# RWKV-7 pair of head groups: in each level's stint all products first, the reads of their PSUM banks behind them, and another order of asking for the banks

## The chip, the core and the metric

The kernel runs on one NeuronCore of a Trainium2 chip. The metric is device time in microseconds (us) from one launch, the median of several runs. TensorE is called PE here, VectorE DVE, ScalarE ACT, GpSimd POOL, SyncE SP. "PEld" is PE's loading of the stationary operand.

## The reference

One decoder block over 256 tokens of width 2048: an input projection, two token mixers side by side (RWKV-7 with 16 heads of 64, and an mLSTM), gates, an output projection, a layer norm, then a mixture of 32 experts and a second layer norm. The change touches the RWKV-7 recurrence only:

```python
def _rwkv7_scan(r, decay, k, v, kk, a):
    # S_t = S_{t-1} (diag(w_t) - kk_t^T (a_t * kk_t)) + v_t^T k_t ;  y_t = S_t r_t
    def step(state, inp):
        r_t, w_t, k_t, v_t, kk_t, a_t = inp
        s_kk = jnp.einsum('bhvk,bhk->bhv', state, kk_t)
        state = (state * w_t[:, :, None, :]
                 - s_kk[..., None] * (kk_t * a_t)[:, :, None, :]
                 + v_t[..., None] * k_t[:, :, None, :])
        return state, jnp.einsum('bhvk,bhk->bhv', state, r_t)
    ...
# and around it
    u = x @ w_in[i]
    y_r = _rwkv7_mixer(u_r, ...); y_m = _mlstm_mixer(u_m, ...)
    mix = (sigmoid(g_r) * (y_r @ w_br[i]) + sigmoid(g_m) * (y_m @ w_bm[i])) @ w_out[i]
    x = _layer_norm(ALPHA * x + mix, ...)
    moe = _hier_moe(x, ...)            # top-1 of 4 groups, top-2 of its 8 experts
    x = _layer_norm(ALPHA * x + moe + ple, ...)
```

## The kernel before

**The front.** The projections run as weight steps on PE. A step takes 256 KB of weights that SP has loaded, ACT rounds them to a high part (line 224) and DVE takes the remainder as a low part (line 225), four steps ahead of PE (`AHEAD = 4`), and PE multiplies by the high part (line 289, 512 columns) and by the low part (line 290, 256 columns), four pairs of L289 and L290 in a step around the change. SP loads the next weights when a raw buffer has been split.

**The mixers in between.** The recurrence and the mLSTM are generators. After each weight step `advance()` first lets a finished projection's evacuation do one piece (L364 on ACT, L366 on DVE, L376 to L378, L940), then runs the next piece of the mixer in front, up to its `yield n`; `n` is how many weight steps pass before the next piece. Such a piece is called a stint here. The order on every engine is therefore the order in which the code is written; nothing reorders it later, and each engine works through its own queue in that order. A tile framework puts in the semaphore waits, by tile of PSUM or SBUF.

**The pair.** The 16 heads are four groups of four heads; the 256 tokens are four chunks of 64. For each group `opening(g)` prepares, for every chunk and head, a 64x64 triangular matrix (`BA`) and a first approximation `Tm` of the inverse of identity plus that matrix. `closing(a, b)` then takes two groups as a pair and doubles the exact block size of the inverse five times for each, in ten levels k = 0 to 9: even k for group a, odd k for group b. A level has two halves, and its second half is done in the stint of the next level, beside the first half of the other group's level:

- first half of level k: 16 products `BA` x `Tm` of 64x64 into columns 0 to 255 of two banks `X[0]`, `X[1]` (L570); four transposes of `Tm` into a bank `pz` (L583); a copy of `pz` to `Gm` by ACT (L584); and a masked copy of the products to `M1` by DVE, one instruction for each bank (L586).
- second half of level k-1: 16 products `Gm` x `M1` into columns 256 to 511 of the same two banks (L562), and `Tm -= ` these, one DVE instruction for each bank (L565).

In levels 0 and 1 there are 16 more products into a bank `px` (L578) with a copy `Xs` by ACT (L580). In the stint k = 10 only the second half of level 9 is left, and the first part of `ending(a)` follows in the same stint: for q = 0 and then q = 1 products into `P[q]` (L608, L613), which ACT and DVE read (L615, L616). There are two pairs, so each of these stints occurs twice in a run. `Gm` and `M1` exist once; `Tm` exists once for each group of the pair (B_66 and B_63 in the rows below).

**The banks.** `bank()` takes the next of four PSUM banks in turn (`bufs=4`); a bank's new owner waits until the old owner's readers are through. `bank2()` gives the projections two double banks of their own (`dps`).

Of a stint's code the order before was: ask for `X[0]` and `X[1]`; products L562; the two subtractions L565; products L570; in levels 0 and 1 products L578 and copy L580; ask for `pz`; transposes L583; copy L584; masks L586.

Of the kernel before, what the change touches and what calls it, by code (L numbers as in the profile page):

```python
# [14 lines left out]
AF = mybir.ActivationFunctionType  # L15
OP = mybir.AluOpType
# [96 lines left out]
def _carve(t, off, *dims, p0=0, p1=128):  # L113
    n = int(np.prod(dims))
    ap = t[p0:p1, off:off + n]
    if len(dims) > 1:
        names = "abcde"[:len(dims)]
        ap = ap.rearrange("p (%s) -> p %s" % (" ".join(names), " ".join(names)),
                          **{m: d for m, d in zip(names, dims)})
    return ap  # L120
# [3 lines left out]
def hybrid_block(ctx: ExitStack, tc: tile.TileContext, xt, xp, vec, cst, sel8, rows, ln1c, pt, w_lora, w_rkv, w_qk,  # L124
                 w_mv, w_o, w_gt, lw, lg1, w_br, w_bm, w_out, ifb, w_rt, b_rt, w_gu0, w_gu2, w_dn, w_pg, out):
    nc = tc.nc
    pe, act, dve, pool, sp = nc.tensor, nc.scalar, nc.vector, nc.gpsimd, nc.sync
# [8 lines left out]
    def bank():  # L136
        return ps.tile([128, 512], FT, name="mps", tag="m", bufs=4)


    def big(i, dt=FT):  # L140

        return sb.tile([128, 4096], dt, name=f"B{i}", tag=f"B{i}")
# [13 lines left out]
    def cst_(name, w=None, o=0):  # L156
        return C[:, _CST[name] + o:_CST[name] + o + (w or 128)]
# [188 lines left out]
    sets = [{n: _carve(*h[n], *d) for n, d in dims.items()} for h in (homes_a, homes_b)]  # L346
# [53 lines left out]
    def evac_mixed(g, w):  # L400

        name, lock, old = (("mu_r", "zr", g - 1), ("mu_k", "zr", g - 1), ("mu_v", "zv", g - 2))[w]
        dst = (zr, zk, zv[:, g % 2])[w]

        def f(p_):
            t = yield from total_slow(p_)
            while free[lock] < old:
                yield
            for c in range(2):
                (shift_chunks if w == 2 else shift_mix)(dst[:, :, c] if w == 2 else dst[:, c], t[:, c],  # L410
                                                        *vm(name, 2 * g + c))
                yield
            if w == (1 if g else 2):
                mixers.append(opening(g))
                if g % 2:
                    mixers.append(closing(g - 1, g))
        return f
# [5 lines left out]
    quarter = lambda p_, o=0: p_[:, o:o + 256].rearrange("p (j n) -> p j n", n=64)  # L423
# [128 lines left out]
    def closing(a, b):  # L552

        ends = [ending(g) for g in (a, b)]
        for k in range(11):
            X = bank(), bank()
            up, down_ = (sets[(k + i) % 2] for i in range(2))
            if k:
                Tm = down_["Tm"]
                for j in range(4):  # L560
                    for c, q in quads:
                        mm(X[q][half[c], 256 + 64 * j:320 + 64 * j], Gm[half[q], j, c, :], M1[half[q], c, j, :],  # L562
                           start=True, stop=True)
                for q in range(2):
                    dve.tensor_tensor(Tm[:, :, q], Tm[:, :, q], quarter(X[q], 256), op=OP.subtract)  # L565
            if k < 10:
                Tm, BA, Xs, vN = (up[n] for n in ("Tm", "BA", "Xs", "vN"))
                for j in range(4):
                    for c, q in quads:
                        mm(X[c][half[q], 64 * j:64 * j + 64], BA[half[c], q, j, 2, :], Tm[half[c], j, q, :], start=True,  # L570
                           stop=True)
                if k < 2:
                    px = bank()
                    for q in range(2):
                        for j in range(4):
                            for c in range(2):
                                o = 256 * q + 64 * j
                                mm(px[half[c], o:o + 64], BA[half[c], q, j, 0, :], vN[half[c], j, half[q]], start=True,  # L578
                                   stop=True)
                    act.activation(Xs.rearrange("p q j n -> p (q j n)"), px, AF.Copy)  # L580
                pz = bank()
                for j in range(4):
                    pe.transpose(pz[:, 128 * j:128 * j + 128], tok(Tm, j), ident)  # L583
                act.activation(Gm.rearrange("p j c n -> p (j c n)"), pz, AF.Copy)  # L584
                for c in range(2):
                    dve.tensor_tensor(M1[:, c], quarter(X[c]), bc(cst_("lv", 64, k // 2 * 64), 4), op=OP.mult)  # L586
                yield Y_LV[k]
            else:
                yield next(ends[0])
        while ends:  # L590
            w = 0
            for e in list(ends):
                n = next(e, 0)
                if not n:
                    ends.remove(e)
                w = max(w, n)
            if w:
                yield w

    def ending(g):  # L600
# [77 lines left out]
        flat8 = lambda a: a.rearrange("p b n -> p (b n)")  # L678
        dve.tensor_reduce(flat8(mean), y, axis=AX.X, op=OP.add)
        dve.tensor_scalar(mean, mean, -1.0 / 64, None, op0=OP.mult)  # L680
# [4 lines left out]
        yield next(wait)  # L685
        dve.tensor_reduce(flat8(rstd), ysq.rearrange("p s h n -> p (s h) n"), axis=AX.X, op=OP.add)
        yield next(wait)
# [558 lines left out]
    x1 = _carve(big(8), 0, 2, 2048)  # L1246
# [567 lines left out]
    for e in range(NE - 2):  # L1814
        g, i = (e + 2) // 4, (e + 2) % 4
# [17 lines left out]
        if over:  # L1833
            pz, ph = pu2[:, 1], pu[:, 0, 256:384]
# [231 lines left out]
```

## Time and profile before

| | us |
|---|---|
| median of 3 runs | 1771.89 (1770.75 to 1774.1) |
| the profiled execution | 1773.26 |
| its span, first to last instruction | 1771.5 |
| PE busy | 1570.8 (89%) |
| DVE busy | 788.2 (44%) |
| ACT busy | 601.8 (34%) |
| granted PE clock, mean | 0.953 |
| first pair's stints k = 0 to 10 | from 176.9 on |
| second pair's last stint k = 10 | starts at 417.99 |

In the timeline a row gives the start in us, the duration in us, engine, line, operation, output and inputs, shapes and the number of instructions merged; a bracket gives the idle time of the engine ahead of it and what ended it. Each 64x64 product stands there as two matrix instructions, so 16 products read "x32". The ends of matrix instructions are modelled, so the steps between starts say more than durations.

### The profile page before, as it was taken

What the parts mean: (1) busy time and instruction counts of PE and PEld (TensorE: products, weight loads), DVE (VectorE), ACT (ScalarE), POOL (GpSimd) and SP (SyncE); (2) the same over time, 40 slices, a digit from 0 to 9 for tenths busy, and PEclk for the clock granted to TensorE, in tenths of its full rate; (3) what the DMA queues carried; (4) which work ended last, traced back from release to release, by engine and by line L of the source; (5) the groups of instructions that cost most, each with busy time, mean ns of one, the idle gap of its engine ahead of it and who ended that gap; (6) DMA issues with size and microseconds to landing.
All of it is one profiled execution on the core that took longest, in us unless ns stands there. A gap on an engine that the chain in (4) does not pass through costs nothing. (4 is left out here: it accounts for less than half of the span.)

```text
span 1771.5 us, 35255 instructions
## 1 busy us (share of the span) xinstructions
PE 1570.8 (89%) x14589; PEld 1090.5 (62%) x14589; DVE 788.2 (44%) x1655; ACT 601.8 (34%) x1122; POOL 25.1 (1%) x39
## 2 busy tenths in 40 slices
PE   7999899999999999999898878797887879877886
PEld 6888788877888888776465455364555334433332
DVE  5577578765775787755231201221201312321315
ACT  5656357643765565444121011111011111111122
POOL 1000000000000000000000000000000000000002
PEclk9999999999999999999999998899999899988888
DMA  7554235432566448867999999999999999999997
GB/s 239 174 167 152 83 113 174 151 111 73 160 187 201 148 149 332 323 226 300 428 425 427 425 426 426 395 428 425 426 426 427 424 425 392 428 424 426 425 427 323
DMA packets 68767, 542.09 MB, mean 306 GB/s; under 512 B 7796, under 2 KB 12292, under 8 KB 42704
## 3 DMA queue, kind: packets, MB, share of 16 engines
q1 hardware_dynamic: 67728, 537.33, 77.1%
q8 instruction: 146, 2.39, 0.6%
q0 software_dynamic: 832, 1.87, 0.4%
q14 instruction: 61, 0.50, 0.1%
HBM read 537.06 MB, written 2.36 MB: 304 GB/s over the span
## 5 line engine op out<-in xcount | busy, mean ns | idle before, releaser
L289 PE MATMUL dps<-B,B 128*128 128x512 f32 x1456 | 530.4, 406 | 11.9 <-DVE B L1204 11.2
L290 PE MATMUL dps<-B,B 128*128 128x256 f32 x1456 | 412.4, 283 | 4.8 <-DVE B L225 4.4
L225 DVE TENSOR_TENSOR B<-B,B 128x512 fp32r<-128x512 f32 (+1 forms) x464 | 312.6, 683 | 195.1 <-ACT B L224 191.0
L224 ACT ACTIVATE B<-B 128x512 fp32r<-128x512 f32 (+1 forms) x464 | 283.6, 622 | 156.9 <-PE dps L289 67.2
L289 PEld LDWEIGHTS dps<-B,B 128*128 128x128 f32 x1456 | 276.7, 190 | 79.7 <-ACT B L224 9.1
L1514 PE MATMUL dps<-B,B 128*32 128x256 f32 x3936 | 252.3, 414 | 64.3 <-DMA B<-in_w_up_dram 29.6
L290 PEld LDWEIGHTS dps<-B,B 128*128 128x128 f32 x1456 | 278.3, 191 | 12.7 <-DVE B L225 10.3
L1514 PEld LDWEIGHTS dps<-B,B 128*32 128x32 f32 x3936 | 134.8, 118 | 185.5 <-issue 43.7
L1519 DVE SCALAR_TENSOR_TENSOR M<-M,dps 128x128 f32<-128x128 f32 x31 | 8.9, 288 | 368.9 <-ACT M L1518 368.9
L1908 ACT ACTIVATE B<-mps 32x512 f32<-32x512 f32 x120 | 70.6, 588 | 180.6 <-PE mps L1534 179.5
L1534 PE MATMUL mps<-B,M 128*32 128x512 f32 x992 | 125.0, 644 | 6.9 <-DMA B<-in_w_down_dram 2.5
L1311 PE MATMUL mps<-B,B 128*128 128x206 f32 (+1 forms) x640 | 112.8, 336 | 0.3 <-DVE B L1300 0.3
L1311 PEld LDWEIGHTS mps<-B,B 128*128 128x128 f32 x640 | 110.6, 190 | 1.4 <-issue 0.8
L1518 ACT ACTIVATE M<-dps 128x128 f32<-128x128 f32 x31 | 8.6, 278 | 270.6 <-PE dps L1514 270.6
L1534 PEld LDWEIGHTS mps<-B,M 128*32 128x32 f32 x992 | 31.0, 116 | 82.6 <-issue 71.5
L297 PE MATMUL dps<-B,B 128*128 128x512 f32 x192 | 76.1, 397 | 1.2 <-DVE B L988 0.8
L299 PE MATMUL dps<-B,B 128*128 128x512 f32 x192 | 75.1, 391 | 0.7 <-DVE B L225 0.7
L298 PE MATMUL dps<-B,B 128*128 128x512 f32 x192 | 74.8, 390 | 0.0
L1590 DVE TENSOR_TENSOR B<-mps,V 128x512 f32<-128x512 f32 (+1 forms) x34 | 21.9, 643 | 86.5 <-PE mps L1584 86.5
L1554 PE MATMUL mps<-B 128*128 128x512 f32 (+1 forms) x128 | 56.7, 595 | 0.7 <-ACT B L1908 0.7
L1514 PE MATMUL dps<-B,C 128*32 128x256 f32 x768 | 46.9, 401 | 7.6 <-DVE C L1591 7.6
L1324 DVE SCALAR_TENSOR_TENSOR C<-C,mps 128x412 f32<-128x412 f32 (+1 forms) x10 | 5.8, 581 | 102.1 <-PE mps L1316 92.0
(511 smaller groups left out, 1554.1 us busy)
## 6 DMA issues: line engine op xcount, KB each, us to landing
B<-in_w_gate_dram SPq DMA_DIRECT2D x62, 2048.0 KB, 19.5
B<-in_w_up_dram SPq DMA_DIRECT2D x61, 2048.0 KB, 21.9
B<-in_w_down_dram SPq DMA_DIRECT2D x60, 2048.0 KB, 21.2
B<-in_w_gt_dram SPq DMA_DIRECT2D x64, 512.0 KB, 3.6
B<-in_w_rkv_dram SPq DMA_DIRECT2D x48, 512.0 KB, 3.6
B<-in_w_pg_dram SPq DMA_DIRECT2D x10, 1854.0 KB, 29.5
B<-in_w_out_dram SPq DMA_DIRECT2D x32, 512.0 KB, 3.8
B<-in_w_qk_dram SPq DMA_DIRECT2D x16, 512.0 KB, 3.6
```

Of the source, the lines that this page charges most:

```text
L224: act.activation(h, src, AF.Copy)
L225: dve.tensor_tensor(wl[i % 4][:, :w], src, h.bitcast(FT), op=OP.subtract)
L289: mm(pt_[:, c], h[:, w], x.rearrange("p a t -> p (a t)"), start=k == 0, stop=False)
L290: mm(pt_[:, c, :256], l[:, w], x[:, 0], start=False, stop=k == nk - 1)
L297: mm(o, mh[:, ts_], h, start=first, stop=False)
L298: mm(o, ml[:, ts_], h, start=False, stop=False)
L299: mm(o, mh[:, ts_], l, start=False, stop=last)
L1311: mm(pp[:, tb], x1T[0][:, k, tb * 128:tb * 128 + 128], w[:, k, :n], start=k == 0 and tb == 0, stop=k == 15 and tb == 1)
L1514: mm(pu[32 * j:32 * j + 32].rearrange("p (a f) -> p a f", a=2), xs[:, 4 * q + k, :], o, start=q == QS[0] and k == 0, stop=q == QS[-1] and ...
L1534: mm(pd[32 * j:32 * j + 32, :], hT_[:, 32 * c:32 * c + 32], w[:, c % 2, 512 * j:512 * j + 512], start=c == 0, stop=c == 3)
L1554: mm(pz, SWT[p0:p1, tb * 128:tb * 128 + 128], yq[p0:p1, o], start=True, stop=True)
L1908: act.activation(yq[32 * i:32 * i + 32, 512 * j:512 * j + 512], pd[32 * j:32 * j + 32, :], AF.Copy)
```

## The change

The stint's code is put in another order, and the three banks are asked for in the order `X[0]`, `pz`, `X[1]`, in all stints, k = 10 too (where `pz` is then not used). All products of a stint (L562, L568 that was L570, L576 that was L578) and the transposes (L579, was L583) come first; then the copy `Gm` (L580, was L584), the masks `M1` (L582, was L586), in levels 0 and 1 the copy `Xs` (L584, was L580), and the two subtractions last (L588, was L565). No instruction is added or removed.

```diff
         for k in range(11):
-            X = bank(), bank()
-            up, down_ = (sets[(k + i) % 2] for i in range(2))
+            x0, pz, x1 = (bank() for _ in range(3))
+            X = x0, x1
+            up, last = (sets[(k + i) % 2] for i in range(2))
             if k:
-                Tm = down_["Tm"]
                 for j in range(4):
                     for c, q in quads:
                         mm(X[q][half[c], 256 + 64 * j:320 + 64 * j], Gm[half[q], j, c, :], M1[half[q], c, j, :],
                            start=True, stop=True)
-                for q in range(2):
-                    dve.tensor_tensor(Tm[:, :, q], Tm[:, :, q], quarter(X[q], 256), op=OP.subtract)
             if k < 10:
                 Tm, BA, Xs, vN = (up[n] for n in ("Tm", "BA", "Xs", "vN"))
                 for j in range(4):
...
                                 mm(px[half[c], o:o + 64], BA[half[c], q, j, 0, :], vN[half[c], j, half[q]], start=True,
                                    stop=True)
-                    act.activation(Xs.rearrange("p q j n -> p (q j n)"), px, AF.Copy)
-                pz = bank()
                 for j in range(4):
                     pe.transpose(pz[:, 128 * j:128 * j + 128], tok(Tm, j), ident)
                 act.activation(Gm.rearrange("p j c n -> p (j c n)"), pz, AF.Copy)
                 for c in range(2):
                     dve.tensor_tensor(M1[:, c], quarter(X[c]), bc(cst_("lv", 64, k // 2 * 64), 4), op=OP.mult)
+                if k < 2:
+                    act.activation(Xs.rearrange("p q j n -> p (q j n)"), px, AF.Copy)
+            if k:
+                for q in range(2):
+                    Tm = last["Tm"]
+                    dve.tensor_tensor(Tm[:, :, q], Tm[:, :, q], quarter(X[q], 256), op=OP.subtract)
+            if k < 10:
                 yield Y_LV[k]
             else:
                 yield next(ends[0])
```

PE's queue in the stint k = 4 of the first pair, with the engines whose semaphores a row waits for, before:

```order
L562 MATMUL mps<-B_66 64x64 [waits DVE_49,Activation_49]
L562 MATMUL mps<-B_66 64x64 [waits PE_49]
L562 MATMUL mps<-B_66 64x64 [waits DVE_49]
L562 MATMUL mps<-B_66 64x64 x13
L570 MATMUL mps<-B_66,B_68 64x64 [waits DVE_49]
L570 MATMUL mps<-B_66,B_68 64x64
L570 MATMUL mps<-B_66,B_68 64x64 [waits DVE_49]
L570 MATMUL mps<-B_66,B_68 64x64 x13
L583 MATMUL mps<-C,B_66 128x128 [waits PE_49]
```

and now:

```order
L562 MATMUL mps<-B_66 64x64 [waits DVE_49,Activation_49]
L562 MATMUL mps<-B_66 64x64 [waits PE_49]
L562 MATMUL mps<-B_66 64x64 [waits DVE_49]
L562 MATMUL mps<-B_66 64x64 x13
L568 MATMUL mps<-B_66,B_68 64x64 [waits DVE_49] x2
L568 MATMUL mps<-B_66,B_68 64x64 x14
L579 MATMUL mps<-C,B_66 128x128 x4
```

The order of PE's work is the same. The first products into each bank waited for DVE in the same stint (the subtraction of that bank); the DVE wait that is left at L568 is for DVE work that stands ahead of this stint's products: the subtraction that wrote this group's `Tm` one stint earlier.

DVE's queue in the stint k = 7 of the first pair, as a difference (`-` before, `+` now):

```order
 L225 TENSOR_TENSOR B_70<-B_69,B_70 128x512 [waits Activation_49]
 L366 TENSOR_TENSOR R<-R,dps 128x512
-L565 TENSOR_TENSOR B_66<-B_66,mps 128x4x64 [waits PE_49] x2
-L586 TENSOR_TENSOR B_66<-mps,C 128x256 [waits DVE_49,PE_49] x2
+L582 TENSOR_TENSOR B_66<-mps,C 128x256 [waits DVE_49,PE_49] x2
+L588 TENSOR_TENSOR B_66<-B_66,mps 128x4x64 x2
 L225 TENSOR_TENSOR B_70<-B_69,B_70 128x512 [waits DMAHW1_49,Activation_49]
 L377 SCALAR_TENSOR_TENSOR B_63<-R,V,B_63 128x4x63 [waits Activation_49]
```

The two masks now stand ahead of the two subtractions; what stands ahead of and behind the four is the same.

PE's queue in the stint k = 10 of the first pair, before:

```order
L562 MATMUL mps<-B_66 64x64 x13
L608 MATMUL mps<-B_68,B_66 64x64 [waits PE_49]
L608 MATMUL mps<-B_68,B_66 64x64 x7
L613 MATMUL mps<-B_66 64x64 [waits DMAHW7_49]
L608 MATMUL mps<-B_68,B_66 64x64 [waits PE_49]
```

and now:

```order
L562 MATMUL mps<-B_66 64x64 x13
L611 MATMUL mps<-B_68,B_66 64x64 [waits DVE_49]
L611 MATMUL mps<-B_68,B_66 64x64 x7
L616 MATMUL mps<-B_66 64x64 [waits DMAHW7_49]
L611 MATMUL mps<-B_68,B_66 64x64 [waits DVE_49]
```

Both halves q = 0 and q = 1 of the ending's first products now wait for DVE. With the third bank asked for in this stint, `P[1]` gets the bank of `X[0]`, which this stint's first subtraction reads; `P[0]` waits for `Tm`, written one stint earlier.

## The prediction

> **What bounds the kernel now.** I read the page first, for where the time of the changed stints lies.
>
> ```profile
> span 1771.5 us, 35255 instructions
> PEclk9999999999999999999999998899999899988888
> DMA  7554235432566448867999999999999999999997
> ```
>
> The stints lie in the fifth, sixth, ninth and tenth slice. There the DMA engines are busy 2 to 4 tenths and PE has its full clock. I then cut the span into stretches (busy us and count of PE, PEld, DVE, ACT, POOL; granted PE clock, DMA share, GB/s).
>
> ```profile
> 176.90:226.50 49.60, 43.77 (x907) 36.30 (x907) 26.40 (x60) 17.64 (x33) 0.00 (x0) 1.00 0.25 76
> 380.00:430.00 50.00, 45.40 (x970) 37.71 (x966) 26.38 (x59) 16.89 (x31) 0.00 (x0) 1.00 0.23 73
> 430.00:760.00 330.00, 322.55 (x1990) 273.18 (x1982) 239.58 (x472) 190.79 (x346) 1.23 (x4) 0.99 0.61 208
> 760.00:1771.50 1011.50, 843.83 (x8175) 477.29 (x8173) 260.91 (x643) 176.30 (x348) 14.17 (x14) 0.92 0.97 406
> ```
>
> Up to 760 us PE sets the pace: 322.55 of 330 us busy behind the pairs, less only in the pairs themselves. From 760 us on the weights' stream does (DMA share 0.97). So time won by PE in a pair brings all of the front forward, and with it the start of the stream. What PE waits for in the pairs stands in the waits (total us, times, longest) and the groups:
>
> ```profile
> PE mps L570 <- DVE B L565: 11.0, 18, 0.9
> L570 PE MATMUL mps<-B,B 64*64 64x64 f32 x640 | 19.5, 227 | 11.0 <-DVE B L565 11.0
> ```
>
> 18 waits: k = 1 to 9 in both pairs. Since the ends of PE's instructions are modelled, 11.0 need not be the whole loss, and I measured from start to start. All engines in the stint k = 3:
>
> ```profile
> 192.37 0.69 DVE L225 TENSOR_TENSOR B<-B,B 128x512 fp32r<-128x512 f32 x1 [1.12 <-ACT B L224]
> 192.44 0.69 PE L562 MATMUL mps<-B 64*64 64x64 f32 x32
> 193.19 0.75 DVE L565 TENSOR_TENSOR B<-B,mps 128x256 f32<-128x256 f32 x2
> 193.66 1.01 PE L570 MATMUL mps<-B,B 64*64 64x64 f32 x32 [0.53 <-DVE B L565]
> 194.61 0.66 PE L583 MATMUL mps<-C,B 128*128 128x128 f32 x4
> 194.64 0.76 DVE L586 TENSOR_TENSOR B<-mps,C 128x256 f32<-128x256 f32 x2 [0.70 <-PE mps L570]
> 195.36 0.60 ACT L584 ACTIVATE B<-mps 128x512 f32<-128x512 f32 x1 [3.03 <-PE mps L583]
> 195.86 0.62 ACT L224 ACTIVATE B<-B 128x512 fp32r<-128x512 f32 x1
> 196.51 0.69 DVE L225 TENSOR_TENSOR B<-B,B 128x512 fp32r<-128x512 f32 x1 [1.12 <-ACT B L224]
> 196.59 0.69 PE L562 MATMUL mps<-B 64*64 64x64 f32 x32
> ```
>
> L562 runs, DVE subtracts from the first bank, and only then may L570 write there; its second bank waits for the second subtraction, which stretches L570 to 1.01. L562 to L583 takes 2.17 us, and the whole stint with its weight step 4.15.
>
> **The change part by part.** *The products.* What two sets of products take with nothing between them is shown where no subtraction stands: at k = 0 (L570, L578, L583) and at k = 10 (L562, L608, L613).
>
> ```profile
> 176.91 0.69 PE L570 MATMUL mps<-B,B 64*64 64x64 f32 x32
> 177.42 1.11 PE L578 MATMUL mps<-B,B 64*64 64x64 f32 x32
> 178.47 0.66 PE L583 MATMUL mps<-C,B 128*128 128x128 f32 x4
> 222.48 0.69 PE L562 MATMUL mps<-B 64*64 64x64 f32 x32
> 222.99 0.65 PE L608 MATMUL mps<-B,B 64*64 64x64 f32 x16
> 223.29 0.75 DVE L565 TENSOR_TENSOR B<-B,mps 128x256 f32<-128x256 f32 x2
> 223.81 0.65 PE L608 MATMUL mps<-B,B 64*64 64x64 f32 x16
> 224.27 0.53 PE L613 MATMUL mps<-B 64*64 64x64 f32 x12
> 224.73 0.50 PE L289 MATMUL dps<-B,B 128*128 128x512 f32 x1
> ```
>
> From 16 undisturbed products of 0.69 us to the next 64x64 products it is 0.51 us (176.91 to 177.42, 222.48 to 222.99). To the 128x128 work behind them it is longer: L578, of 1.11, starts 1.05 ahead of L583, and L613, of 0.53, 0.46 ahead of L289, so 0.06 to 0.07 below the duration, which makes 0.62 after 0.69. (The new pair of neighbours, L568 and L579, has no row: the ends are 0.51, as among 64x64 products, and 0.69, the whole duration; 0.62 is from the nearest rows.) A stint k = 2 to 9 then takes 0.51 + 0.62 = 1.13 from L562 to the transposes, and k = 1, with L576 (was L578) between, 0.51 + 0.51 + 1.05 = 2.07.
>
> *Beside it, the page "TensorEngine Tiling (Array Packing)" of the Trainium skill says under Key Properties that a change of tiling mode drains PE. The rows above agree: 0.62 into the 128x128 work against 0.51 within 64x64. By a chip without that drain the 16 stints would each give 0.11 more, 1.8 us in all.*
>
> What these stints take now, besides k = 3: the last of the 16, the k = 1 of the first pair, and the four whose wait is longer than 0.53.
>
> ```profile
> 413.84 0.69 PE L562 MATMUL mps<-B 64*64 64x64 f32 x32
> 416.01 0.66 PE L583 MATMUL mps<-C,B 128*128 128x128 f32 x4
> 181.83 0.69 PE L562 MATMUL mps<-B 64*64 64x64 f32 x32
> 184.93 0.66 PE L583 MATMUL mps<-C,B 128*128 128x128 f32 x4
> 210.65 1.01 PE L570 MATMUL mps<-B,B 64*64 64x64 f32 x32 [0.90 <-DVE B L565]
> 215.10 1.01 PE L570 MATMUL mps<-B,B 64*64 64x64 f32 x32 [0.84 <-DVE B L565]
> 219.55 1.01 PE L570 MATMUL mps<-B,B 64*64 64x64 f32 x32 [0.83 <-DVE B L565]
> 406.76 1.01 PE L570 MATMUL mps<-B,B 64*64 64x64 f32 x32 [0.91 <-DVE B L565]
> ```
>
> Twelve take 2.17; the four take 0.37, 0.31, 0.30 and 0.38 more, since evacuation work of DVE stood ahead of the subtraction. Together 16 x 2.17 + 1.36 = 36.1. Now 16 x 1.13 = 18.1, which leaves **18.0**. The two k = 1: 2 x (3.10 - 2.07) = **2.1**.
>
> *DVE's order.* Masks first, subtractions behind. With T the start of the transposes (k = 3: 194.61), the masks start at T + 0.03, both subtractions end at about T + 0.03 + 0.76 + 0.75 = T + 1.54. The next stint's L562 comes, as before, 1.98 after T (194.61 to 196.59), its L568 at T + 2.49. L562 needs the masks (T + 0.79) and `Gm` (T + 0.75 + 0.60 = T + 1.35); L568 needs the subtractions. All are early, by 0.6 us at the least. The weights' split comes behind, as before: L225 starts at T + 1.90, when DVE is just free. What the new period of 1.98 + 1.13 = 3.11 us must hold on DVE is 0.75 + 0.76 + 0.69 = 2.2 us, in a stint with an evacuation up to 0.7 more (the row below), which fits. Cost 0; if this cover were gone, PE would stand at L568 with the transposes and the next step's L289 queued behind, and ACT's L224, which waits for freed weight buffers, behind those.
>
> ```profile
> L366 DVE TENSOR_TENSOR R<-R,dps 128x512 f32<-128x512 f32 x24 | 16.3, 680 | 0.8 <-ACT R L364 0.8
> ```
>
> *ACT's order.* In levels 0 and 1 `Gm` comes ahead of `Xs`, 0.6 us earlier than now; two weight steps follow, so nobody feels it. `Xs` is read in the ending only. No DMA moves against the steps, and nothing on POOL.
>
> *Banks.* `pz` of a stint gets the bank of the last stint's `X[0]`, whose reader ended at T + 1.54 at the latest, 1.5 us ahead of the transposes. At k = 10 the products for q = 1 get this stint's `X[0]` bank: the subtraction starts at 223.29 and its first half ends some 0.4 later, 0.1 ahead of the second L608 at 223.81. Hidden here with little to spare; bound 0 to 0.7 (one L366 ahead of it), twice; I take 0.
>
> Sum: 18.0 + 2.1 = **20.1 us**, between 17 (0.15 in each of the 18 stints and 0.4 at the two k = 10 together given back; 0.69 in place of 0.62 alone costs 1.1) and 21.9 (0.51 in place of 0.62). The profiled execution took 1773.26, 1.8 more than its span, which makes 1753.2; the runs' median is 1.4 lower, 1771.89, which makes **1751.8**, and I say 1752.
>
> **The rivals.** *Only the listed wait goes* (0.08): 11.0 us, 1760.9. That would be so if L570's 1.01 and L562's 0.69 were their own pace. The k = 0 row with 0.51 between starts speaks against it.
>
> *The end does not move* (0.05): 1771.9. The chain's end is the stream of the experts' weights, and if its start were set by something other than the front, PE's gain would become waiting there:
>
> ```profile
> PE dps L1514 <- DMA B<-in_w_up_dram: 29.6, 13, 3.1
> ```
>
> Against it: the DMA share is 0.25 and 0.61 in the stretches ahead of 760, so the stream is not running yet, and the buffers it goes to are the front's.
>
> *Slower: the subtraction that is now last in DVE's queue holds L568* (0.04). It has 0.95 us to spare (T + 1.54 against T + 2.49), and what a stint saves is 2.17 - 1.13 = 1.04, so it decides from 2.0 us of lateness in every stint: with 2.4 us, 16 x 0.4 = 6.4 us slower, some 1778. That takes the weights' split and two evacuation pieces between masks and subtractions; the queue has nothing between them. Such waits are real here: L570 waits 0.53 although it writes columns that the subtraction doesn't read, and a bank's next owner will too.
>
> *On this the page "PSUM — Partial Sum Buffer" of the Trainium skill, under "PSUM bank collisions raise a hardware error", has engines kept apart by bank and quadrant, not by address. The wait at L570 agrees.*
>
> **How the numbers follow.** Forecast 0.83, the others 0.08, 0.05 and 0.04, in this order. The forecast alone spans 1748.5 (21.9, and the median a little low, as the runs differ by 3 us) to 1756; up to 1761 it takes in the second case and holds 9 in 10 on these chances. I leave it there, since I have no row for the new order itself. About 0.2% (3.5 us) is what a measurement here can tell from no change: faster 0.91 (the forecast, the 11 us case), same 0.05, slower 0.04.
>
> **What would show it.** Right: no wait of PE for the subtraction in the 18 stints; L562 to L568 0.51 and L568 to L579 near 0.62; periods near 3.1 us instead of 4.15; the first pair's k = 10 some 10 us earlier, the second pair's some 20. Wrong: a wait at L568 or the next L562; L579 a full us behind L568; L611 for q = 1 waiting at k = 10; or a front that is 20 us shorter with the stream's first wait where it was.

## The result, and the profile after

The changed kernel took 1755.98 us, the median of 4 runs (1753.15 to 1756.09), against 1771.32 us (1770.6 to 1774.1, 4 runs) for the kernel before, timed beside it. The ratio is 0.9907, with a 95% interval of 0.989 to 0.9924: 15.3 us faster. The forecast was 1752.0 us. Its profiled execution took 1755.92 us.

The page of the changed kernel: the span, the granted clock and the DMA share in 40 slices.

```profile
span 1754.2 us, 35260 instructions
PEclk9999999999999999999999999898998889988988
DMA  7554345533565458868999999999999998999997
```

In the stints' slices (the fifth and sixth, the ninth and tenth) DMA reads 3, 4, 3 and 3 tenths, where it read 2, 3, 3 and 2 before (the prediction's "2 to 4" is one too many at its upper end). Stretches of the changed kernel, in the columns used in the prediction; the first two lie in the pairs, the last is mostly the stream:

```profile
176.90:216.50 39.60, 39.60 (x897) 34.15 (x896) 26.30 (x61) 17.18 (x32) 0.00 (x0) 1.00 0.31 97
370.00:409.00 39.00, 39.00 (x962) 33.73 (x964) 24.93 (x57) 16.11 (x30) 0.00 (x0) 1.00 0.31 97
745.00:1754.00 1009.00, 832.76 (x8145) 467.97 (x8144) 257.69 (x638) 172.85 (x343) 14.17 (x14) 0.93 0.97 405
```

PE is now busy through the whole of both pairs (39.60 of 39.60 us in the first, where it was 43.77 of 49.60). The groups of the changed kernel's products, subtractions and masks (busy us, mean ns, idle time ahead and what ended it):

```profile
L568 PE MATMUL mps<-B,B 64*64 64x64 f32 x640 | 13.0, 219 | 0.0
L562 PE MATMUL mps<-B 64*64 64x64 f32 x640 | 13.9, 224 | 0.0
L582 DVE TENSOR_TENSOR B<-mps,C 128x256 f32<-128x256 f32 x40 | 15.1, 419 | 9.2 <-PE mps L568 9.1
L588 DVE TENSOR_TENSOR B<-B,mps 128x256 f32<-128x256 f32 x40 | 14.8, 412 | 0.1
```

The 11.0 us that PE waited for the subtraction are gone, and nothing stands in their place. The products' busy time fell as well, from 19.5 to 13.0 us: 6.5 us of what was listed as work had been waiting between the two banks. Another 3 us lie behind L562: L568 starts 0.52 us after it in the rows below, 0.17 ahead of the modelled end of its 0.69, while L570's listed wait was counted from that end on (192.44 + 0.69 + 0.53 = 193.66). 18 times 0.17 is 3.1, and 11.0, 6.5 and 3.1 make 20.6 us. The timeline of a stint of the changed kernel and the start of the next, PE and DVE:

```profile
189.36 0.69 PE L562 MATMUL mps<-B 64*64 64x64 f32 x32
...
189.88 0.65 PE L568 MATMUL mps<-B,B 64*64 64x64 f32 x32
...
190.46 0.66 PE L579 MATMUL mps<-C,B 128*128 128x128 f32 x4
190.56 0.76 DVE L582 TENSOR_TENSOR B<-mps,C 128x256 f32<-128x256 f32 x2 [0.58 <-PE mps L568]
...
191.23 0.74 DVE L588 TENSOR_TENSOR B<-B,mps 128x256 f32<-128x256 f32 x2
...
192.36 0.69 DVE L225 TENSOR_TENSOR B<-B,B 128x512 fp32r<-128x512 f32 x1 [0.38 <-ACT B L224]
...
192.43 0.69 PE L562 MATMUL mps<-B 64*64 64x64 f32 x32
...
192.95 0.65 PE L568 MATMUL mps<-B,B 64*64 64x64 f32 x32
```

From L562 to the transposes it is 1.10 us (was 2.17), and the period is 3.07 us (was 4.15). The subtractions end at 191.97, 0.98 us before the next L568. The timeline of PE in the stints k = 1 and k = 10 of the first pair:

```profile
180.91 0.69 PE L562 MATMUL mps<-B 64*64 64x64 f32 x32
181.43 0.65 PE L568 MATMUL mps<-B,B 64*64 64x64 f32 x32
181.89 1.11 PE L576 MATMUL mps<-B,B 64*64 64x64 f32 x32
182.94 0.66 PE L579 MATMUL mps<-C,B 128*128 128x128 f32 x4
...
210.83 0.69 PE L562 MATMUL mps<-B 64*64 64x64 f32 x32
211.35 0.65 PE L611 MATMUL mps<-B,B 64*64 64x64 f32 x16
211.81 0.53 PE L616 MATMUL mps<-B 64*64 64x64 f32 x12
212.16 0.65 PE L611 MATMUL mps<-B,B 64*64 64x64 f32 x16
```

The second L611 follows without a wait. How much shorter the pairs' part of the front is, is read best from the first L562 (k = 1 of the first pair) to the last (k = 10 of the second). The row of that line by its source (duration in ns, then the first and last start), of the kernel before and then of the changed one:

```profile
L562 PE MATMUL mps<-B x640: 218/218/268, 181.8 to 418.5; 64*64 64x64 f32 x160
```

```profile
L562 PE MATMUL mps<-B x640: 218/218/268, 180.9 to 396.9; 64*64 64x64 f32 x160
```

That is 236.7 us before and 216.0 now: **20.7 us** shorter. (The 0.9 us by which the first L562 is earlier lie ahead of the change.) So the front gave what was forecast, and a little more, while the time fell by 15.3 us only. Where the difference went is the question of the experiments. It is not lost in the front. The product into a spare bank in the router, the last work ahead of the experts, starts at 823.7 before and at 802.1 now, and the last down product at 1760.6 and 1742.4. The rows are again by source, first of the kernel before, then of the changed kernel:

```profile
L1366 PE MATMUL mps<-C x32: 275/372/421, 823.7 to 828.9; 128*128 128x128 f32 x32
L1534 PE MATMUL mps<-B,M x992: 589/592/1063, 844.3 to 1760.6; 128*32 128x512 f32 x199
```

```profile
L1369 PE MATMUL mps<-C x32: 275/275/356, 802.1 to 805.6; 128*128 128x128 f32 x32
L1537 PE MATMUL mps<-B,M x992: 589/592/1062, 822.5 to 1742.4; 128*32 128x512 f32 x199
```

The router is 21.6 us earlier (20.7 and the 0.9), the last product 18.2. From the one to the other, the stream of the experts' weights, it is 936.9 us before and 940.3 now: 3.4 us of the gain are missing at the end of this stretch, none at its start. Behind the last product 0.9 more are missing (11.8 us to the end of the span, where it was 10.9). So the two profiled executions differ by 17.3 us (1773.26 less 1755.92), and the medians of all runs by 15.3.

### The profile page after: what moved, and what is told of

Its sections match the earlier page's. It is cut to its first block, busy times and chain, and to the rows that moved or that the text cites. A ratio compares the mean times of both kernels' runs of the same rounds, so it can differ in the third digit from the quotient of the medians.

```text
span 1754.2 us, 35260 instructions
## 1 busy us (share of the span) xinstructions
PE 1555.4 (89%) x14589; PEld 1079.6 (62%) x14589; DVE 786.9 (45%) x1655; ACT 600.8 (34%) x1122; POOL 25.1 (1%) x39
## 5 line engine op out<-in xcount | busy, mean ns | idle before, releaser
L289 PE MATMUL dps<-B,B 128*128 128x512 f32 x1456 | 528.9, 405 | 11.2 <-DVE B L1207 10.4
L290 PE MATMUL dps<-B,B 128*128 128x256 f32 x1456 | 411.1, 282 | 4.8 <-DVE B L225 4.4
L225 DVE TENSOR_TENSOR B<-B,B 128x512 fp32r<-128x512 f32 (+1 forms) x464 | 312.5, 682 | 184.6 <-ACT B L224 178.1
L289 PEld LDWEIGHTS dps<-B,B 128*128 128x128 f32 x1456 | 275.7, 189 | 79.8 <-ACT B L224 9.2
L1517 PE MATMUL dps<-B,B 128*32 128x256 f32 x3936 | 247.1, 407 | 65.8 <-DMA B<-in_w_up_dram 33.4
L290 PEld LDWEIGHTS dps<-B,B 128*128 128x128 f32 x1456 | 277.0, 190 | 12.7 <-DVE B L225 10.3
```

The lines of the kernel that those rows point to most:

```text
L225: dve.tensor_tensor(wl[i % 4][:, :w], src, h.bitcast(FT), op=OP.subtract)
L289: mm(pt_[:, c], h[:, w], x.rearrange("p a t -> p (a t)"), start=k == 0, stop=False)
L290: mm(pt_[:, c, :256], l[:, w], x[:, 0], start=False, stop=k == nk - 1)
L1517: mm(pu[32 * j:32 * j + 32].rearrange("p (a f) -> p a f", a=2), xs[:, 4 * q + k, :], o, start=q == QS[0] and k == 0, stop=q == QS[-1] and ...
```

## The experiments

Two theories explain the missing part. **Theory A**: the front's 20.7 us go through to the end one to one, and the stream varies by several us from one execution to the next, whatever kernel runs; then a repetition, or a variant with an equally short front, should lie as often above 20 us as below. **Theory B**: an earlier stream is a slower stream, and part of the gain is lost there every time. Beside that it is asked which part of the change does the work, and what DVE's new order would cost if its cover were gone. In the diffs the starting point is the changed kernel, but for the two where it is said.

**The changed kernel again.** No edit.

> The changed kernel again, for more runs and a second trace. The front was 20.7 us shorter up to the second pair's last stint (21.6 by the clock of the trace), the end only 17.3 us earlier in the profiled execution. Theory A (the stream of the experts' weights loses or gains a few us by chance in each execution): front again 20 to 21 us shorter, medians from 1751 to 1756, and a second trace has its losses at other places or none. Theory B (the stream loses some 4 us because it starts earlier): the same loss at the same place, median 1755 to 1756.5, every execution within 1 us of it.

Measured: 1750.97 us (1750.04 to 1754.0) against 1773.52 before, ratio 0.9873 (0.9849 to 0.9897): 22.6 us faster, with the same front (181.8 to 397.4, 215.6 us). The two results of the one kernel differ by 7 us in their gain, and the first was at the low end. The median, at the lower end of theory A's range, speaks against theory B. The trace does not: its stream takes 940.7 us and has its loss at the same place as the first one, as theory B expected of it (more on that below).

**The order of the work without the order of the banks.**

```diff
-            x0, pz, x1 = (bank() for _ in range(3))
-            X = x0, x1
+            X = bank(), bank()
...
+                pz = bank()
                 for j in range(4):
                     pe.transpose(pz[:, 128 * j:128 * j + 128], tok(Tm, j), ident)
```

> The order of the work as changed, the banks asked for as before (X[0], X[1], then pz; none at k = 10). Theory 1 (the order alone removes the waits; the bank order is worth nothing, since the only reader in the way, the subtraction from X[0], ends some 0.4 us ahead of the next stint's L562): stint k = 2 to 9 1.09 us from L562 to the transposes as in the changed kernel, no wait of PE for a subtraction, time within 2 us of the changed kernel. Rival 2 (the bank order carries part of the gain): the next stint's second product into the bank of the old X[0] waits 0.3 to 0.5 us for the subtraction, 16 times, 5 to 8 us slower than the changed kernel.

Measured: 1752.79 us (1750.5 to 1756.15), ratio 0.988 (0.9856 to 0.9905): 20.7 us faster. The front is 215.7 us long, and PE waits for no subtraction.

**The order of the banks without the order of the work.** Taken from the kernel before:

```diff
-            X = bank(), bank()
+            x0, pz, x1 = (bank() for _ in range(3))
+            X = x0, x1
...
-                pz = bank()
```

> Only the order in which the three banks are asked for is changed, the work stands as before. Theory 1: PE goes on waiting 0.53 to 0.9 us for the subtraction in 18 stints, 11.0 us in the waits, time within 2 us of the kernel before (1769 to 1774). Rival 2 (the banks carry part of the gain): the wait is shorter, 3 to 10 us faster than before.

Measured: 1775.42 us (1770.07 to 1782.83) against 1773.52, ratio 1.0012 (0.9993 to 1.0031): no change, though the median lies 1.4 us above the range expected. Its waits have the old row, at the old size:

```profile
PE mps L571 <- DVE B L566: 10.9, 18, 0.9
```

So the whole gain comes from the order of the work. Which bank the transposes get is worth nothing that can be measured, alone or with the new order.

**All products first, but the subtractions ahead of the masks.**

```diff
                 act.activation(Gm.rearrange("p j c n -> p (j c n)"), pz, AF.Copy)
+                if k:
+                    for q in range(2):
+                        t_ = last["Tm"]
+                        dve.tensor_tensor(t_[:, :, q], t_[:, :, q], quarter(X[q], 256), op=OP.subtract)
                 for c in range(2):
                     dve.tensor_tensor(M1[:, c], quarter(X[c]), bc(cst_("lv", 64, k // 2 * 64), 4), op=OP.mult)
...
-            if k:
+            if k == 10:
                 for q in range(2):
```

> As the changed kernel, but DVE does the two subtractions ahead of the two masks, still behind all products. Theory 1 (what counted was that the subtractions stood between the two sets of products; DVE's order behind them is covered by the weight step): masks end 0.75 us later, 1.54 us after the transposes start, 0.4 us ahead of the next L562; no wait of PE, time within 2 us of the changed kernel. Rival 2 (the order of masks and subtractions matters, the cover is gone): L562 waits for the masks in most stints, 0.2 to 0.5 us each, 4 to 9 us slower than the changed kernel.

Measured: 1751.18 us (1748.35 to 1753.71), ratio 0.987 (0.9843 to 0.9898): 22.3 us faster, front 216.0 us, no waits. DVE's order behind the products doesn't matter. What counts is that no read of the two banks stands between the two sets of products.

**The new order in the first pair only.** The second pair keeps the order before (`a` is the number of the pair's first group, 0 in the first pair).

```diff
+            if a == 0:
+                x0, pz, x1 = (bank() for _ in range(3))
+                X = x0, x1
+            else:
+                X = bank(), bank()
...
+            if k and a:
+                for q in range(2):
+                    Tm = last["Tm"]
+                    dve.tensor_tensor(Tm[:, :, q], Tm[:, :, q], quarter(X[q], 256), op=OP.subtract)
...
-            if k:
+            if k and not a:
```

> The new order and bank order in the first pair only, the second pair as before. Theory A (each pair brings its PE time, some 10.3 us, and the front's gain goes through to the end one to one): the second pair's L562 starts some 10.7 us earlier than before and its waits are back (9 of them, 5.5 us), time halfway between the two kernels, 1759 to 1765. Theory B (part of the gain is lost in the stream because it starts earlier): nearer to the kernel before, 1765 to 1769, or nearer to the changed one.

Measured: 1761.96 us (1759.69 to 1767.73) against 1775.52, ratio 0.9918 (0.9895 to 0.9942): 13.6 us faster. Its wait, and its L562:

```profile
PE mps L575 <- DVE B L570: 5.1, 9, 0.9
L565 PE MATMUL mps<-B x640: 218/218/268, 180.4 to 406.4; 64*64 64x64 f32 x160
```

The front is 226.0 us long, 10.7 less than before, half of 20.7 within a few tenths. The time fell by 2.9 us more than that.

**The same time put back elsewhere in the front.** 64 products of 128x128 with nothing to wait for, behind the pairs and ahead of the next phase of PE's work; they compute nothing that is used.

```diff
     drain()
+    idle_ps = bank()
+    for i in range(64):
+        mm(idle_ps[:, :128], ident, cst_("ones"), start=True, stop=True)
```

> The changed kernel with 64 idle products of 128x128 put on PE between the projections and the output half of the front, where no mixer runs; the 16 such products that the kernel has anyway took 3.5 us, so 64 take about 14 us. Theory A: the end moves by as much, some 14 us slower than the changed kernel, 1765 to 1769. Theory B (the end is set by the stream, whose start does not follow the front): under 5 us slower.

The row of these products (first and last start):

```profile
L1221 PE MATMUL mps<-C x128: 272/275/275, 653.5 to 667.7; 128*128 128x128 f32 x128
```

By this row they hold the front up by 14.2 us. From the last L562 to the spare product it is 418.4 us here and 403.4 to 407.3 in the ten other traces, so 11 to 15 us arrive at the start of the stream. Measured: 1764.3 us (1761.82 to 1766.26) against 1775.52, ratio 0.9931 (0.9906 to 0.9956): 11.2 us faster. That is a little under theory A's 1765 to 1769, and 8 to 13 us above the changed kernel's three results, so it is not theory B's "under 5 us slower". The pairs' part is 215.7 us here, 21.0 shorter than before, so 21.0 - 14.2 = 6.8 would be one to one. That errs on the other side than the first result: here less of the loss arrived, there less of the gain.

**Two more DVE instructions between masks and subtractions**, in the stints k = 1 to 9. Each writes the maximum of a half of `Tm` and itself back, so the values stay.

```diff
+            for i in range(2 if 0 < k < 10 else 0):
+                t_ = last["Tm"][:, :, i % 2]
+                dve.tensor_tensor(t_, t_, t_, op=OP.max)
             if k:
                 for q in range(2):
```

> The changed kernel with two more DVE instructions (Tm = max(Tm, Tm), the result is the same) between the masks and the subtractions of each stint k = 1 to 9, about 0.4 us each. Theory 1 (the subtraction has 0.95 us to spare before the next stint's L568): it ends some 2.35 us after the transposes start, L568 comes at 2.49; no wait or one under 0.1 us, time within 2 us of the changed kernel. Rival (no cover): 0.8 us in each of 16 stints, 13 us slower.

Measured: 1753.81 us (1752.14 to 1756.08), ratio 0.9874 (0.9851 to 0.9897): 21.7 us faster, front 215.7 us, no wait. The lateness lies within the 0.98 us that the subtraction has to spare.

**Six of them.** The same edit with 6 for 2.

> As the one with two, but six more DVE instructions, about 2.4 us. Theory 1: the subtraction ends some 3.9 us after the transposes start, so the next L568 waits 1.4 to 1.5 us in the 16 stints that come one weight step after the last: PE waits for the subtraction some 23 us in all, about 24 us slower than the changed kernel, and so a little slower than the kernel before (1774 to 1779). It would show the price of the rival in which the subtraction, now last, comes too late. Rival (DVE's work here is never waited for): as the changed kernel.

Measured: 1771.37 us (1768.14 to 1776.14) against 1775.52, ratio 0.9983 (0.9971 to 0.9996). Its waits of PE, its L562, and the timeline of a stint:

```profile
PE mps L568 <- DVE B L591: 8.9, 14, 0.9
PE mps L614 <- DVE B L591: 1.4, 2, 0.8
L562 PE MATMUL mps<-B x640: 218/218/268, 180.2 to 413.9; 64*64 64x64 f32 x160
```

```profile
187.45 2.09 DVE L587 TENSOR_TENSOR B<-B 128x256 f32<-128x256 f32 x6
...
188.64 0.69 PE L562 MATMUL mps<-B 64*64 64x64 f32 x32
189.46 0.74 DVE L591 TENSOR_TENSOR B<-B,mps 128x256 f32<-128x256 f32 x2
...
189.92 1.02 PE L568 MATMUL mps<-B,B 64*64 64x64 f32 x32 [0.58 <-DVE B L591]
...
190.87 0.66 PE L579 MATMUL mps<-C,B 128*128 128x128 f32 x4
```

The six take 2.09 us, 0.35 each, where 0.4 each was expected, and the time stays below the 1774 to 1779 us expected with it. The subtraction now starts when this stint's L562 is already at work, and L568 waits for it again, 0.58 us and a stretch to 1.02. The front is 233.7 us long: 17.7 of the 20.7 us are given back, not 24 as with 0.4 each. The products are still ahead in PE's queue, and PE's other waits in the pairs are those of the changed kernel (1.1 us for L225, 0.3 behind the pairs' products); what brings the time back is the late read. That is the mechanism of the prediction's slower rival, close to the point from which it was to decide; the kernel as a whole stays a little faster than before.

**The changed kernel a third time.** No edit.

> The changed kernel a third time, beside the kernel before on the same chip. So far it was 15.3 us faster in one comparison and 22.6 in another. Theory A (its worth is the front's 20.7 us, and the rest is the stream's scatter of a few us from execution to execution): 18 to 23 us faster, with the front up to the second pair's last L562 20 to 21 us shorter again. Theory B (about 15 is what comes through): 14 to 17 us.

Measured: 1754.7 us (1752.95 to 1758.33) against 1773.39, ratio 0.9901 (0.9884 to 0.9919): 18.7 us faster.

**What the ten results say together.** The gain of the front (236.7 us less its length, for the padded kernel also less 14.2) beside the gain in the medians, each against the kernel before timed with it:

| kernel | front, us | time, us |
|---|---|---|
| banks only | -0.1 | -1.9 |
| six more on DVE | 3.0 | 4.2 |
| changed, with idle products | 6.8 | 11.2 |
| first pair only | 10.7 | 13.6 |
| changed | 20.7 | 15.3 |
| changed, third time | 20.8 | 18.7 |
| order of work only | 21.0 | 20.7 |
| two more on DVE | 21.0 | 21.7 |
| subtractions first | 20.7 | 22.3 |
| changed, second time | 21.1 | 22.6 |

The differences of the two columns have a mean of 0.3 us and a spread of 2.8; the changed kernel's three results have a mean of 18.9, the six with the short front 20.2. Theory A holds within this: the gain passes one to one, and a single comparison of medians is good to some 3 us here. A loss of 5 us every time, theory B, would show in all six, and doesn't; a loss of a us or two would not be seen. Three cautions belong to the table. The ten rows have only four timings of the kernel before (1771.32, 1773.52 four times, 1775.52 four times, 1773.39), so the rows that share one move together. Two of the 95% intervals leave out the front's gain, that of the first result (13.5 to 19.5 us) and that of the padded kernel (7.8 to 16.7), so an interval from one set of runs doesn't hold all the scatter. And the stream is not the only part that varies: the way from the last L562 to the spare product, without the padded kernel, takes 403.4 to 407.3 us.

**Where the stream's 3.4 us lie.** The spare and down rows of the third time of the changed kernel, and of the one with the banks only:

```profile
L1369 PE MATMUL mps<-C x32: 275/275/356, 804.0 to 807.6; 128*128 128x128 f32 x32
L1537 PE MATMUL mps<-B,M x992: 589/592/1062, 824.4 to 1740.5; 128*32 128x512 f32 x199
```

```profile
L1366 PE MATMUL mps<-C x32: 275/275/356, 822.5 to 826.1; 128*128 128x128 f32 x32
L1534 PE MATMUL mps<-B,M x992: 592/592/1062, 842.9 to 1763.2; 128*32 128x512 f32 x199
```

The stream takes 936.5 us in an execution with the early start, and 940.7 in one with the late start. So neither length belongs to one start alone. In all four executions the stream is full (423 to 425 GB/s) in its first 640 us on the whole, and not in the 80 us behind them. Those 80 us, of the kernel before, the changed one, its third time, and the banks only:

```profile
1463.70:1543.70 80.00, 73.66 (x894) 33.94 (x890) 20.15 (x51) 13.55 (x29) 0.00 (x0) 0.98 0.97 408
```

```profile
1442.10:1522.10 80.00, 72.75 (x864) 33.49 (x866) 22.53 (x54) 13.25 (x28) 0.00 (x0) 0.97 0.94 388
```

```profile
1444.00:1524.00 80.00, 73.65 (x894) 34.25 (x890) 20.16 (x51) 13.55 (x29) 0.00 (x0) 0.98 0.97 406
```

```profile
1462.50:1542.50 80.00, 72.84 (x873) 33.48 (x875) 22.31 (x54) 13.25 (x28) 0.00 (x0) 0.97 0.91 378
```

20 and 30 GB/s less over 80 us, at some 425, are 3.8 and 5.6 us of transfer: of these four, the two long streams are the two with less here. They are 3.4 and 3.8 us longer, so the first loss fits and the second is more than is missing. What holds the transfers up there is in SP's waits in the same 80 us, for the kernel before and then the changed one:

```profile
SPq L1103 <- PE dps L1514: 39.3, 5, 25.2
```

```profile
SPq L1106 <- PE dps L1517: 41.7, 5, 27.5
```

SP may issue the next load when PE has read the buffer; it waits 2.4 us longer for PE in the changed kernel's first execution, 3.8 longer in the one with the banks only (43.1), and 39.3 as before in the third time of the changed kernel. So in some executions PE reaches this place late.

The seven other traces show that this is a part of the story only. Four of them (the second time, the order of work only, the subtractions first, the first pair only) have long streams, 940.7 to 942.7 us, and the same loss: 377 to 388 GB/s in these 80 us, with 42.2 to 44.2 us of SP's wait. Six more on DVE has a short stream (936.4) and no loss. But the two more on DVE and the padded kernel have 939.8 and 940.1 us with 405 and 408 GB/s and a wait of 39.2 and 39.3: their 3 us lie elsewhere, and where was not looked for. The loss at this place occurs in four of the six kernels with the short front and in one of the three with the old one or nearly so, and the streams' means are 940.4 and 938.0 us. With one trace of each kernel that shows no effect of the start, and does not exclude one of a us or two. (In six of the ten results the profiled execution was the longest of its runs.)

Why PE comes late was not settled. A candidate is the clock granted to PE, as in these rows of the changed kernel's first execution, some 70 us ahead of that stretch (the clock is the third number from the end):

```profile
1362.30:1370.30 8.00, 6.69 (x31) 3.60 (x35) 2.64 (x10) 0.66 (x2) 0.00 (x0) 0.50 1.01 428
1370.30:1378.30 8.00, 6.86 (x60) 2.26 (x54) 0.75 (x1) 3.42 (x6) 0.00 (x0) 0.95 0.72 303
```

Eight microseconds at half the clock, and behind them a hole in the transfers. But dips of the clock occur in every execution of the stream: in the third time of the changed kernel the clock falls to 0.50 at the same distance from the spare product too, twice for nearly 7 us, and no 2 us there move less than 393 GB/s. No run held the clock fixed, so this is an argument and not shown.

*The Trainium skill, in the page "TensorE: Matmul & The Clock Gate", section "What's actually happening", says that the gate has only the two states 4/8 and 8/8. The trace agrees: in windows of 1 us the two rows read 0.50 eight times, then 0.59 once and 1.00 in the next two, so the 0.95 is a mean over both states.*

## Why the prediction was right, and where it was not

*That PE sets the front's pace and the front the stream's start*: right. PE is busy in all of both pairs now, the router is 21.6 us earlier and the experts' first products with it. The rival that the end does not move is out.

*That the whole stint is worth more than the listed wait*: right, and it is what the forecast stands on. The listed 11.0 us are gone, and 20.7 were gained at the front. The rest was hidden by modelled ends: a second wait within L570's duration (the groups' 19.5 us fell to 13.0), and some 3.1 us between the start of L568 and the modelled end of L562. The rival with 11.0 us would have left the front at 225.7 us long; it is 216.0.

*The term of the products*, 18.0 us: 18.6 measured. L562 to L568 takes 0.52 us in the rows above (0.51 forecast). L568 to L579 takes 0.58 (0.62 forecast, between 0.51 and 0.69). So 16 stints of 1.095 us, the mean of 1.09 and 1.10, are 17.5 in place of 18.1. The two k = 1 take 2.03 instead of 2.07 and give the forecast 2.1. The sum, 18.6 + 2.1 = 20.7, is what the front shows.

*By the Trainium skill's page "TensorEngine Tiling (Array Packing)", Key Properties, a change of tiling mode drains PE. The rows fit it: the step from 64x64 to 128x128 work is 0.06 us longer here (0.58 against 0.52), about half of the 0.11 that was worked out beforehand. Whether the 0.06 is a drain, or comes from the other operands, no run takes apart.*

*DVE's order at no cost*: right in every step. By T (190.46) the subtractions were to end at T + 1.54, the next split to start at T + 1.90 and L568 at T + 2.49; in the rows it is T + 1.51, T + 1.90 and T + 2.49. The runs with two and with six more instructions show both sides of the limit: with 0.35 us for each, two stay within the 0.98 us to spare, and six, 2.09 us, bring the period from 3.07 to some 4.20 (4.18 to 4.21 where no evacuation comes between), which is 2.09 less 0.98 within 0.02.

*The point from which the slower rival decides*, 2.0 us of lateness: right for the stint. At 2.09 us the period is 4.20 against 4.15 before. The kernel as a whole is still some 3 us ahead there, since the stints k = 1 and k = 2 of both pairs, with two weight steps ahead of them, keep their gain (1.07 us each: 2.03 and 1.09 from L562 to the transposes, as in the changed kernel). The mechanism is real, and it was improbable here because nothing stands between masks and subtractions.

*ACT's order, the banks and the two k = 10 at no cost*: right. There is no wait at the second L611; and the order of the banks is worth nothing in either order of the work.

*The last step, from the front to the time*: the profiled execution less the front's sum was to be the new time. Here the prediction was off: 15.3 us arrived, where 20.1 were forecast, so the measured 1755.98 us lies 4.0 above the 1752.0. The step takes one execution of a stream of 940 us as its length, to the tenth. The profiled execution of the kernel before had one of the shortest streams (936.9), and that of the changed kernel an ordinary one (940.3; the others lie between 936.4 and 942.7). No term for this stood in the sum. The range covered it for other reasons: 1755.98 lies just within the forecast's own 1756, an end that stood for small costs in the stints (17 us in place of 20.1), and these measured nothing; up to 1761 the second rival was allowed for. That the first timing stayed inside was partly luck. Over the six comparisons with the short front, 20.2 us arrived on average. So the size of the front's gain was right, and the first timing came out low by an amount that timings vary by, on both sides: 1771.32 is the lowest of the four timings of the kernel before, and 1755.98 the highest of the three of the changed one.

## What to carry to other kernels

When one engine's work is split by another engine's read of the same PSUM bank, put all writes of the bank first and all reads behind them, and measure what it is worth from start to start: the wait that a profile lists was here about half (11.0 of 20.7 us). Before the reads are put last, work out how long they may be late (here 0.98 us) and what stands ahead of them on their engine; beyond that, the wait comes back at full price. And where the end lies behind a long stretch with another bound, compare the stretch that was changed by itself, and the total only over several timings.

## What was not expected of the hardware

The stream of weights, the same instructions in every kernel here, took 936.4 to 942.7 us from execution to execution, with no clear relation to when it started. In six of the eleven traces a part of it lies in one place, where SP waits for PE (41.7 to 44.2 us in the 80 us shown, against 39.2 to 39.3) and the transfers fall to 377 to 388 GB/s, from 404 to 408. The step from 128x128 to 64x64 work is longer by 0.10 us than one within 128x128 work, and the step back by 0.06 than one within 64x64 work: the products L562 start 0.21 us behind the last L290, where L289 starts 0.11 us behind an L290 within the weight step in the changed kernel's timeline of PE:

```profile
191.88 0.27 PE L290 MATMUL dps<-B,B 128*128 128x256 f32 x1
191.99 0.40 PE L289 MATMUL dps<-B,B 128*128 128x512 f32 x1
192.22 0.28 PE L290 MATMUL dps<-B,B 128*128 128x256 f32 x1
```

The L562 at 192.43 stands in the timeline shown above. Whether that 0.10 us belongs to the change of tile or to what the products load was not tried.
